# Seven half-size products for the second feed-forward matmul of a decoder layer, with sums formed by adding DMAs

## The chip, the core and the metric

The kernel runs on one core of one Trainium2 chip. TensorE (PE) multiplies, VectorE (DVE), ScalarE (ACT) and GpSimd (POOL) do the rest of the arithmetic, and DMAs are issued from the queues of SyncE (SP), POOL and, rarely, ACT. The metric is the device time of one execution in microseconds.

## The reference

One decoder layer on 1024 prompt tokens and 8 x 8 sampled tokens (1088 tokens in all), in float32, model width 1024, feed-forward width 2816:

```python
proj = rmsnorm(x, norm1_g) @ w_in            # q, k, v, glu_a, glu_b, gate_a, gate_b
branch_a = attend(q, k, v, mask, sinks) @ w_o_attn           # window 128, 16 heads
u = glu_a * jax.nn.sigmoid(glu_b)                            # conv module, 31 taps
branch_b = silu(layernorm(dwconv_valid(u_ext, conv_b_w, conv_b_bias))) @ w_pb
h = x + (sigmoid(gate_a) * branch_a + sigmoid(gate_b) * branch_b) @ w_out
up = rmsnorm(h, norm2_g) @ w_up                              # 1024 x 5632
gate, val = jnp.split(dwconv_valid(up_ext, ffn_conv_w, ffn_conv_b), 2, axis=-1)
y = h + (silu(gate) * val) @ w_down                          # 2816 x 1024, changed here
```

The outputs are the normed `y` and the new caches and conv states.

## The kernel before

Activations lie transposed: 128 channels on the partitions, tokens along the free axis. Every float32 operand is split into a rounded part and a rest (`h`, `l`; `split_ps` does it with one ACT copy and one DVE subtract), and a product is three matmuls (`mm3`): high by high, high by low, low by high. Weights come as units of 128 x 1024 from `wall` through two `wraw` buffers (`w_load`, on SP) and are split into `whi` and `wlo` (`w_split`).

The stages follow one another: norm and input projections (`phase_x`), 44 weight units in the order `SEQUENCE`, most of them a stream of 72 matmuls, with attention units woven in between by an agenda (`plan`, `tick`) and the 31-tap convolution as background work on DVE (`conv`); the projections of the two branches and their output (`phase_y`, `phase_z`); then the feed-forward. In its first product (`ffn_up`), channel groups 3 to 21 already use seven products of half size in place of eight: `plan_pair` forms the sums of weight blocks on DVE as it goes, and `pair` adds the results. Each group's gated result goes to DRAM (`d_g`, from POOL). The second product (`down`, `ffn_down`) takes the 22 groups in six lots (`GROUPS`), keeps the output `H` in SBUF and adds each lot to it; the last lot also does the final norm (`final`, `tail`).

The program's text gives a priority, not the order: the scheduler places each instruction on its engine's queue when it reckons that its inputs and its buffer are there, the text's order deciding among those that are ready, and `later` lowers the priority. An engine's queue then runs strictly in the order found. At most eight DMAs of SP and eight of POOL are under way, each queue by eight semaphores in turn. So a DMA without inputs, as one from an input tensor to DRAM, can be placed far ahead of its place in the text. Before the change one such pair of DMAs was tied down by hand:

```python
if f == 2:
    with tc.issue_after(z.ins):
        nc.gpsimd.dma_start(a["o_kwp"], a["kpT"][:, :, :, NT:])
        nc.gpsimd.dma_start(a["o_vwp"], a["vp"][:, NT:, :])
```

Names used below: `xl` the low half of the normed input, `u` the conv module's buffers (two), `gt` the gates' buffers (two) on their way to DRAM, `p` the softmax tiles (two), which a POOL copy of `nsink` opens.

Of the kernel before, what the change touches and what calls it, by code (L numbers as in the profile page):

```python
# [9 lines left out]
ALU = mybir.AluOpType  # L10
# [33 lines left out]
GROUPS = (2, 4, 4, 4, 4, 4)  # L44
# [29 lines left out]
def weight_order():  # L74
    order, count = [], {}
    gates = [(kind, i) for i in range(KT) for kind in ("ga", "gb")]
    for w in SEQUENCE:
        n = count[w] = count.get(w, -1) + 1
        if w == "g":
            order.append(gates.pop(0))  # L80
        elif w[0] == "q":
            order.append(("q", (int(w[1]), n)))
        elif w[0] == "k":
            order.append(("k", int(w[1])))
        else:
            order.append((w, n))
    assert not gates
    n_in = len(order)
    order += [("o", m) for m in range(KT)]
    order += [("pb", m) for m in range(KT)]  # L90
    order += [("out", m) for m in range(KT)]
    for f in range(NF):
        order += [("up", f), ("up", NF + f)]
    order += [("dn", f) for f in range(NF)]
    groups = [list(range(sum(GROUPS[:n]), sum(GROUPS[:n + 1]))) for n in range(len(GROUPS))]
    return order, groups, n_in
# [16 lines left out]
class Build:  # L113
    def __init__(self, tc, a):
        self.tc, self.nc, self.a = tc, tc.nc, a
        self.order, self.groups, self.n_in = weight_order()
# [18 lines left out]
    def w_load(self):  # L135
        i = len(self.w_raw)
        if i < len(self.order):
# [5 lines left out]
    def w_split(self):  # L143
        if len(self.w_hl) < len(self.order):
# [25 lines left out]
    def weight(self, what, ahead=1):  # L170
# [3 lines left out]
        while len(self.w_raw) < min(i + 3, len(self.order)):  # L174
# [358 lines left out]
    def run(self):  # L533
        nc, tc, a = self.nc, self.tc, self.a
        es = ExitStack()
        with es:
# [8 lines left out]
            self.d_g = self.t(dp, [NF, P, FW], "d_g")  # L545
# [22 lines left out]
    def derive(self):  # L568
# [7 lines left out]
        nc.vector.tensor_scalar(self.nsrow, self.c("srow", 0, 2), -1.0, None, ALU.mult)  # L576

# [3 lines left out]
    def phase_x(self):  # L581
# [222 lines left out]

        for n, (kind, i) in enumerate(self.order[:self.n_in]):
            if n < FIRST:
                continue
            if n == self.n_in - LAST_GATES:
# [66 lines left out]
    def phase_z(self, s_es, sh, sl):  # L875
# [102 lines left out]
        H, h_es = self.ffn_up(hh, hl, mp)  # L978
        m_es.close()
        self.ffn_down(H, h_es)  # L980


    def ffn_up(self, hh, hl, mp):
# [12 lines left out]
        first = n_up + 2 * PLAIN  # L996

# [3 lines left out]
        def raw_slot(i):  # L1001
            if first <= i < n_up + 2 * NF and (i - first) // 2 % 2:
                return ft, "wraw2"
            return self.wp, "wraw"

        def slot(i):
            if i < n_up:
                return old_slot(i)
            if i < first:
                return (ft, ("wraw2", "wraw2")) if i == first - 1 else (self.wp, (i - first) % 2)  # L1010
            return ((self.wp, ("wlo0", "whi1")), (ft, ("wraw2", "wraw2")))[i - n_dn]

        old_slot, self.slot = self.slot, slot
        self.raw_slot, self.w_stop = raw_slot, first
        gt = {}
# [23 lines left out]
        def up_conv(f, st, ss):  # L1039
            nc.gpsimd.tensor_copy(co[:, f, 0:2], st[:, SEQ:SEQ + 2])  # L1040
            nc.gpsimd.tensor_copy(co[:, f, 2:].rearrange("p (b t) -> p b t", b=NB), ss[:, :, NT:])
            acc = self.t(ft, [P, AW], "acc", bufs=3)
            nc.scalar.activation(acc, st[:, 0:AW], AF.Identity, bias=fb(f), scale=fw(f, 0))  # L1043
            for k in (1, 2):
                nc.vector.scalar_tensor_tensor(acc, st[:, k:k + AW], fw(f, k), acc, ALU.mult, ALU.add)  # L1045
            return acc

        def finish(f, both):
            with self.later(UP_LATER):
                ga = up_conv(f, *both[0][:2])  # L1050
                nc.scalar.activation(ga, ga, AF.Silu)
                va = up_conv(NF + f, *both[1][:2])
                nc.vector.tensor_tensor(va, va, ga, ALU.mult)
                nc.gpsimd.dma_start(self.d_g[f, :, 0:AW], va)
# [14 lines left out]
        def sums():  # L1069
            add = lambda o, x, y, op=ALU.add: nc.vector.tensor_tensor(o, x, y, op)  # L1070
            for j in range(2):
                for kk in range(0, KT // 2, 2):
                    ks = slice(kk, kk + 2)

                    def word(c, y):
                        r = self.t(ft, [P, 2, QW], "s", bufs=4)
# [4 lines left out]
                    add(r11, r12, r11, ALU.subtract)  # L1081
                    add(r12, r22, r12, ALU.subtract)
                    add(r22, r22, r11, ALU.subtract)
                    add(r21, r21, r22, ALU.subtract)
# [3 lines left out]

        ring = {"n": 0, "tiles": []}
# [5 lines left out]
        preps = []  # L1095

        def plan_pair(f):
            i = n_up + 2 * f
            hw = DM // 2
            live = {}  # L1100

            def raws():
                while len(self.w_raw) < min(i + 4, len(self.order)):
                    self.w_load()
                ra, rb = self.w_raw[i:i + 2]
                live.update(a11=ra[:, :hw], a12=ra[:, hw:], a21=rb[:, :hw], a22=rb[:, hw:])

            def make(name, x, y, op):
                def go():
                    s = live[name] = self.t(ft, [P, 2 * QW], "s", bufs=4)[:, :hw]  # L1110
                    nc.vector.tensor_tensor(s, live[x], live[y], op)
                return go

            def split(name, before=None):
                def go():
                    if name == "a11":
                        raws()
                    if before:
                        before()
                    w = self.t(self.wp, [P, DM], ("whi0", "wlo0", "whi1", "wlo1")[ring["n"] % 4], F32R, bufs=1)  # L1120
                    ring["n"] += 1
                    self.split_ps(w[:, :hw], w[:, hw:], live[name])
                    ring["tiles"].append((w[:, :hw], w[:, hw:]))
                return go

            preps.extend([
                split("a11"),
                split("s1", make("s1", "a21", "a22", ALU.add)),
                split("s2", make("s2", "s1", "a11", ALU.subtract)),
                split("s4", make("s4", "a12", "s2", ALU.subtract)),  # L1130
                split("s3", make("s3", "a11", "a21", ALU.subtract)),
                split("a12"), split("a22")])

        def prep(n):
            while ring["n"] < min(n, len(preps)):
                preps[ring["n"]]()

        def pair(f):
# [4 lines left out]
            plus = lambda d, s: nc.vector.tensor_tensor(d, d, s, ALU.add)  # L1143
            seq = [
                ("A", "11", True, pg, 0, copy), ("E", T1, True, pv, 2, copy), ("A", T2, False, pg, 2, copy),
                ("E", "22", False, pg, 2, plus), ("A", T3, False, pv, 2, plus), ("C", "21", True, pg, 0, plus),
                ("A", T4, False, pv, 0, copy)]
            for n, (bank, b, fresh, parts, c, op) in enumerate(seq):
                prep(base + n + 1 + AHEAD)
                if f == NF - 1 and n == 4:  # L1150
                    self.w_hl += [None] * (n_dn - len(self.w_hl))
                    self.w_stop = len(self.order)
                    for _ in self.groups[0]:
                        self.w_load()
                        self.w_split()
                wh, wl = ring["tiles"][base + n]
                for j in range(2):
# [8 lines left out]
                    for d, r in parts(c + j):  # L1166
                        op(d, r(ps))  # L1167
            finish(f, both)

        for f in range(PLAIN, NF):  # L1170
            plan_pair(f)
# [5 lines left out]
        self.w_used = self.order.index(("dn", 0))  # L1177
        for f in range(PLAIN, NF):
            pair(f)
            if f == NF - 4:  # L1180
                for x in self.groups[0]:
                    t = self.t(ft, [P, AW], "acc", bufs=3)[:, :T]
                    gt[x] = self.g_load(x, t, *(self.t(mp, [P, T], f"m{y}{2 + x}0", F32R) for y in "hl"))
        nc.gpsimd.dma_start(a["o_cf"], co)
        t_es.close()
        h_es = ExitStack()
        H = self.t(pool(h_es, "hd", "left"), [P, KT, T], "H")
        self.down(0, H, gt, None)
        f_es.close()
        return H, h_es  # L1190


    def g_load(self, f, va, h, l):
        self.nc.sync.dma_start(va[:, :SEQ], self.d_g[f, :, :SEQ])
        self.nc.sync.dma_start(va[:, SEQ:].rearrange("p (b t) -> p b t", b=NB),
                               self.d_g[f, :, SEQ + 2:].rearrange("p (b t) -> p b t", t=FROW)[:, :, :NT])
        self.split_ps(h, l, va)
        return h, l

    def down(self, n, H, gt, dt, ahead=None):  # L1200
        nc, g, last = self.nc, self.groups[n], n == len(self.groups) - 1
        ws = [self.weight(("dn", f), len(g) - 1 - x) for x, f in enumerate(g)]
        for c, (o, w) in enumerate(TAIL_CHUNKS if last else CHUNKS):
            if c == 1 and ahead:
                ahead()
            ssq = self.t(dt, [P, 384], "fssq", bufs=2) if last else None
            for m in range(KT):
                ms = slice(m * P, (m + 1) * P)
                ps = self.bank(("mm", "aux")[m % 2])
                for x, f in enumerate(g):  # L1210
                    h, l = gt[f]
                    self.mm3(ps[:, :w], ws[x][0][:, ms], ws[x][1][:, ms], h[:, o:o + w], l[:, o:o + w],
                             x == 0, x == len(g) - 1)
                hs = H[:, m, o:o + w]
                if n == 0:
                    nc.scalar.copy(hs, ps[:, :w])
                else:
                    nc.vector.tensor_tensor(hs, hs, ps[:, :w], ALU.add)
                if n == 1:
# [213 lines left out]
```

## Time and profile before

| what | value |
|---|---|
| time, median of 3 runs (lowest to highest) | 1707.12 us (1704.47 to 1707.89) |
| profiled execution: span from first to last instruction | 1704.2 us; its time outside the span is not given |
| PE busy | 1679.8 us, 11440 matmuls |
| DVE, ACT, POOL busy | 1281.4, 850.0, 246.4 us |
| moved by DMA | 172.18 MB, mean 101 GB/s |
| mean PE clock granted | 0.996 |

Busy time is the time in which an engine runs an instruction; matmuls overlap, so a busy PE says only that there are no gaps. DMA share is the part of the 16 DMA engines' time in which they move packets; in a short window it can read above 1. A copy from DRAM to DRAM counts its bytes once in GB/s. Line numbers are those of the kernel that the row belongs to.

### The profile page before, as it was taken

What the parts mean: (1) busy time and instruction counts of PE and PEld (TensorE: products, weight loads), DVE (VectorE), ACT (ScalarE), POOL (GpSimd) and SP (SyncE); (2) the same over time, 40 slices, a digit from 0 to 9 for tenths busy, and PEclk for the clock granted to TensorE, in tenths of its full rate; (3) what the DMA queues carried; (4) which work ended last, traced back from release to release, by engine and by line L of the source; (5) the groups of instructions that cost most, each with busy time, mean ns of one, the idle gap of its engine ahead of it and who ended that gap; (6) DMA issues with size and microseconds to landing.
All of it is one profiled execution on the core that took longest, in us unless ns stands there. A gap on an engine that the chain in (4) does not pass through costs nothing.

```text
span 1704.2 us, 29288 instructions
## 1 busy us (share of the span) xinstructions
PE 1679.8 (99%) x11440; PEld 1661.6 (98%) x11440; DVE 1281.4 (75%) x2253; ACT 850.0 (50%) x1729; POOL 246.4 (14%) x430
## 2 busy tenths in 40 slices
PE   9999999999999999999999999999999999999998
PEld 8999899999999999999999999999999999999998
DVE  8899999999579986755447977777777773754436
ACT  7534577733588736963233535444444455311112
POOL 1210112130011111100000441222222220000000
PEclk9999999999999999999999999999999999999999
DMA  6122213232211274553344132222222223853103
GB/s 208 42 51 79 65 46 113 80 123 63 75 44 56 76 255 144 172 172 125 122 131 135 53 123 77 77 77 77 77 77 77 90 66 125 271 140 103 52 1 106
DMA packets 104347, 172.18 MB, mean 101 GB/s; under 512 B 44512, under 2 KB 70512, under 8 KB 104192
## 3 DMA queue, kind: packets, MB, share of 16 engines
q1 hardware_dynamic: 90352, 124.88, 24.5%
q0 software_dynamic: 13424, 45.15, 7.4%
q8 instruction: 90, 1.47, 0.3%
q14 instruction: 49, 0.40, 0.1%
q10 hardware_dynamic: 432, 0.27, 0.1%
HBM read 124.74 MB, written 47.50 MB: 101 GB/s over the span
## 4 chain that ended last, share of the span: by engine, by line
PE 83%; DVE 10%; ACT 3%; issue 2%; DMA 1%; POOL 0%; SPq 0%; DVEq 0%; ACTq 0%; POOLq 0%
PE mm L182 20%; PE mm L184 20%; PE mm L183 20%; PE aux L184 6%; PE aux L183 6%; PE aux L182 6%; DVE c L456 2%; DVE bt L456 2%; PE aux L342 1%; PE aux L354 1%; PE aux L355 1%; PE aux L332 1%; PE aux L333 1%; DMA xr<-xT 1%; DVE wlo L164 1%
## 5 line engine op out<-in xcount | busy, mean ns | idle before, releaser
L182 PE MATMUL mm<-xh,whi 128*128 128x384 f32 (+1 forms) x920 | 306.3, 333 | 0.4 <-ACT whi L163 0.3
L183 PE MATMUL mm<-xl,whi 128*128 128x384 f32 (+1 forms) x920 | 300.7, 327 | 0.2 <-DVE xl L246 0.2
L184 PE MATMUL mm<-xh,wlo 128*128 128x384 f32 (+1 forms) x920 | 300.3, 327 | 0.0
L182 PEld LDWEIGHTS mm<-xh,whi 128*128 128x128 f32 x920 | 172.9, 188 | 2.0 <-ACT whi L163 0.9
L183 PEld LDWEIGHTS mm<-xl,whi 128*128 128x128 f32 x920 | 173.0, 188 | 1.6 <-DVE xl L246 0.7
L184 PEld LDWEIGHTS mm<-xh,wlo 128*128 128x128 f32 x920 | 172.7, 188 | 0.1
L163 ACT CAST whi<-wraw 128x1024 fp32r<-128x1024 f32 (+1 forms) x91 | 90.0, 993 | 161.6 <-PE aux L183 82.8
L164 DVE TENSOR_TENSOR wlo<-wraw,whi 128x1024 fp32r<-128x1024 f32 (+1 forms) x91 | 104.3, 1151 | 44.7 <-ACT whi L163 44.4
L1045 DVE SCALAR_TENSOR_TENSOR acc<-st,fc,acc 128x1104 f32<-128x1104 f32 x88 | 119.8, 1364 | 4.7 <-ACT acc L1043 3.9
L182 PE MATMUL mm<-mh,whi 128*128 128x272 f32 x368 | 106.6, 290 | 0.0
L183 PE MATMUL mm<-ml,whi 128*128 128x272 f32 x368 | 106.1, 288 | 0.0
L184 PE MATMUL mm<-mh,wlo 128*128 128x272 f32 x360 | 104.1, 289 | 0.0
L456 DVE SCALAR_TENSOR_TENSOR bt<-u,consts,bt 128x513 f32<-128x513 f32 x120 | 89.9, 750 | 0.6
L456 DVE SCALAR_TENSOR_TENSOR c<-sm,hsum,c 128x512 f32<-128x512 f32 x120 | 89.6, 747 | 0.6
L456 DVE SCALAR_TENSOR_TENSOR c<-u,consts,c 128x512 f32<-128x512 f32 x112 | 83.6, 747 | 0.2
L182 PE MATMUL mm<-gh,whi 128*128 128x384 f32 (+3 forms) x240 | 78.1, 326 | 3.4 <-ACT gh L211 3.4
L183 PE MATMUL mm<-gll,whi 128*128 128x384 f32 (+3 forms) x240 | 78.5, 327 | 0.7 <-DVE gll L212 0.7
L184 PE MATMUL mm<-gh,wlo 128*128 128x384 f32 (+3 forms) x240 | 78.5, 327 | 0.0
L184 PE MATMUL aux<-gh,wlo 128*128 128x384 f32 (+3 forms) x240 | 78.2, 326 | 0.0
L183 PE MATMUL aux<-gll,whi 128*128 128x384 f32 (+3 forms) x240 | 78.2, 326 | 0.0
L182 PE MATMUL aux<-gh,whi 128*128 128x384 f32 (+3 forms) x240 | 78.0, 325 | 0.0
L182 PE MATMUL mm<-th,whi 128*128 128x272 f32 x240 | 70.1, 292 | 2.4 <-ACT st L1167 2.2
(382 smaller groups left out, 5292.0 us busy)
## 6 DMA issues: line engine op xcount, KB each, us to landing
wraw<-wall SPq DMA_DIRECT2D x131, 512.0 KB, 4.0
d_g<-acc POOLq DMA_DIRECT2D x22, 552.0 KB, 5.1
gr<-d_g SPq DMA_DIRECT2D x20, 512.0 KB, 5.2
ga<-d_ga SPq DMA_DIRECT2D x8, 544.0 KB, 4.5
gb<-d_gb SPq DMA_DIRECT2D x8, 544.0 KB, 3.7
mar<-d_ma SPq DMA_DIRECT2D x8, 544.0 KB, 5.6
xr<-xT SPq DMA_DIRECT2D x32, 136.0 KB, 2.4
d_h<-H POOLq DMA_DIRECT2D x4, 1088.0 KB, 5.9
```

What stands on the lines that cost most here:

```text
L163: self.nc.scalar.copy(h[:, z], r[:, z])
L164: self.nc.vector.tensor_tensor(l[:, z], r[:, z], h[:, z].bitcast(F32), ALU.subtract)
L182: mm(ps, wh, xh, start=first, stop=False, skip_group_check=more)
L183: mm(ps, wh, xl, start=False, stop=False, skip_group_check=more)
L184: mm(ps, wl, xh, start=False, stop=last, skip_group_check=more)
L332: nc.tensor.matmul(ps[:, j, :], q[g][:, h, qs], kd[g][:, keys], start=True, stop=False)
L333: nc.tensor.matmul(ps[:, j, :], q[g][:, h, qs], kl[g][:, keys], start=False, stop=True)
L342: nc.tensor.transpose(ps[:, h * P:(h + 1) * P], pt[:, h, kb * P:(kb + 1) * P], self.ident)
L354: nc.tensor.matmul(av, v, ph, start=kb == kbs[0], stop=False)
L355: nc.tensor.matmul(av, v, pl, start=False, stop=kb == kbs[-1])
L456: mac = lambda o, x, w: nc.vector.scalar_tensor_tensor(o, x, w, o, ALU.mult, ALU.add)
L1045: nc.vector.scalar_tensor_tensor(acc, st[:, k:k + AW], fw(f, k), acc, ALU.mult, ALU.add)
```

## The change

Of the 22 groups of the second product, 20 are taken as 10 pairs. A pair's 256 x 1024 weights are cut in 2 x 2 blocks (group by half of the columns), the 256 x 1088 operand in 2 x 2 blocks (group by half of the tokens), and seven products of sums of blocks replace the eight of blocks. The ten pairs run in four rounds (`ROUNDS`) of 2, 3, 3 and 2 pairs; in each round, four blocks of 128 output columns (and the same in the other half) take seven products of 272 columns twice. The last two groups go as before.

The weight sums are no longer formed on DVE but by DMA, for both products: `folds` copies blocks of `wall` to the seven slots of a pair in DRAM (SP) and then adds blocks in three steps (POOL, `accum_op`). The text steps it once per stream of the input projections for the first product (`d_wu`, 19 pairs) and once per group of the feed-forward for the second (`d_wd`, 10 pairs). The operand's sums are formed in `finish` by one DVE sum and adding DMAs into `d_x`. The results of the rounds are added by DMA to `h` in DRAM (`d_h`), from where `H` is loaded for the last two groups and the final norm.

```diff
-GROUPS = (2, 4, 4, 4, 4, 4)
+ROUNDS = ((0, 1), (2, 3, 4), (5, 6, 7), (8, 9))
+NP = 10
+LAST = (20, 21)
+HT = T // 2
+FOLD_FROM = 8
...
+    def folds(self, out, units):
...
+        def put(eng, n, x, slots, **kw):
+            d = out[7 * n + slots.start:7 * n + slots.stop:slots.step or 1].rearrange("x p c -> p x c")
+            eng.dma_start(d, x[:, None, :].to_broadcast([P, d.shape[1], hw]), **kw)
...
+        def plain(n):
+            a, b, c, d = of(n)
+            put(sync, n, a, slice(0, 1))
+            put(sync, n, a, slice(2, 5))
+            put(sync, n, d, slice(1, 7, 5))
+            put(sync, n, b, slice(5, 6))
+
+        def add(n, which, slots):
+            put(gpsimd, n, of(n)[which], slots, accum_op=ALU.add)
+
+        steps = (plain, lambda n: add(n, 2, slice(1, 5)), lambda n: add(n, 3, slice(2, 4)), lambda n: add(n, 1, slice(3, 4)))
+        count = out.shape[0] // 7
+        for at in range(count + len(steps) - 1):
+            for k, step in enumerate(steps):
+                if 0 <= at - k < count:
+                    step(at - k)
+            yield
...
+        folds = self.folds(self.d_wu, lambda n: (n_up + 2 * (n + PLAIN), n_up + 2 * (n + PLAIN) + 1, False))
         for n, (kind, i) in enumerate(self.order[:self.n_in]):
...
+            if n >= FOLD_FROM:
+                next(folds, None)
...
         def finish(f, both):
...
-                nc.gpsimd.dma_start(self.d_g[f, :, 0:AW], va)
...
+                nc.vector.tensor_tensor(s, o[:, :HT], o[:, HT:], ALU.add)
+                x = self.d_x[f // 2].rearrange("x p t -> p x t")
+                halves = o.rearrange("p (x t) -> p x t", x=2)
+                if f % 2:
+                    nc.gpsimd.dma_start(x[:, 5:7], halves)
+                    nc.gpsimd.dma_start(x[:, 2:5:2], o[:, None, HT:].to_broadcast([P, 2, HT]), accum_op=ALU.add)
+                    nc.gpsimd.dma_start(x[:, 3], s, accum_op=ALU.add)
+                else:
+                    nc.gpsimd.dma_start(x[:, 0:5:4], halves)
+                    nc.gpsimd.dma_start(x[:, 1:4], s[:, None, :].to_broadcast([P, 3, HT]))
...
+        def load_two():
...
+                nc.sync.dma_start(r.rearrange("p (x c) -> p x c", x=n), self.d_wu[2 * d:2 * d + n].rearrange("x p c -> p x c"))
...
+                nc.sync.dma_start(l.bitcast(F32).rearrange("p (x c) -> p x c", x=7),
+                                  self.d_wd[f:f + 7, :, m * P:(m + 1) * P].rearrange("x p c -> p x c"))
...
+        folds = self.folds(self.d_wd, lambda n: (n_dn + 2 * n, n_dn + 2 * n + 1, True))
         for f in range(PLAIN, NF):
-            pair(f)
+            next(folds, None)
+            pair(f, hook)
...
+            for n, (bank, fresh) in enumerate((("A", 1), ("E", 1), ("A", 0), ("E", 0), ("A", 0), ("C", 1), ("A", 0))):
...
+                        self.mm3(ps, wh[:, ws], wl[:, ws], x[:, :HT][:, js], x[:, HT:][:, js],
+                                 bool(fresh) and i == 0, i == len(blk[r, m]) - 1, not fresh)
...
+                    nc.gpsimd.dma_start(self.d_h[row, :, half * HT:(half + 1) * HT], ev[d], accum_op=ALU.add)
```

The order on SP right after the load of u for the second conv group. Before (`wraw_948` is the weight unit of the eighth stream):

```order
L603 DMA u_944<-cbT 128x8x30
L140 DMA wraw_948<-wall 128x1024
L140 DMA wraw_1039<-wall 128x1024
L803 DMA masks_942<-masks 128x640
L140 DMA wraw_1187<-wall 128x1024
```

After (`wraw_952` is the same unit; the first row here is the last of 23 copies that stand between it and u_948):

```order
L593 DMA d_wu_64<-wall 128x2x512
L145 DMA wraw_952<-wall 128x1024
L593 DMA d_wu_64<-wall 128x512 x2
L593 DMA d_wu_64<-wall 128x3x512
L145 DMA wraw_1043<-wall 128x1024
```

Plain copies of `d_wu` stand between the weight loads from here on, up to eight ahead of each; all 76 are placed before wraw_2038, the load that was wraw_1991.

The order on POOL where the first softmax tiles are opened (the two copies from `nsink`). Before:

```order
L630 DMA o_cbp<-u_1492 128x30
L631 DMA o_cbs<-u_1492 1024x1x30
L480 DMA d_c_59<-u_944 128x64
L479 DMA d_c_59<-u_944 128x1024
L722 DMA o_vp<-gt_1959 128x256
L601 MEMSET u_2381 128x30
L602 MEMSET u_2381 128x2
L298 COPY p_1998<-nsink_81 128x4
```

After, in a row from the same output DMA of the third u buffer to the same copy:

```order
L671 DMA o_cbp<-u_1511 128x30
L672 DMA o_cbs<-u_1511 1024x1x30
L593 DMA d_wu_64<-wall 128x512
L593 DMA d_wu_64<-wall 128x2x512
L593 DMA d_wu_64<-wall 128x512 x2
L485 DMA d_c_59<-u_948 128x64
L484 DMA d_c_59<-u_948 128x1024
L763 DMA o_vp<-gt_1992 128x256
L642 MEMSET u_2442 128x30
L643 MEMSET u_2442 128x2
L303 COPY p_2045<-nsink_85 128x4
```

All 57 adds into `d_wu` stand ahead of that copy, the first of them right after the first gate write at the kernel's start.

The order on PE where the stream of the next weight unit begins (`mm_2391` before, `mm_2452` after, writing its first PSUM bank). `kd`, `kl`, `q` are the keys and queries of attention scores, `pth` and `ptl` the turned softmax tile, `sp` the softmax tile of the sampled tokens being turned, `av` the result. Before:

```order
L405 MATMUL aux_2413<-consts_74,sp_2345 128x128
L406 MATMUL aux_2413<-consts_74,sp_2345 128x128
L182 MATMUL mm_2391<-xh_17_101,whi_216_2188 128x384
L183 MATMUL mm_2391<-xl_18_102,whi_216_2188 128x384
L184 MATMUL mm_2391<-xh_17_101,wlo_217_2189 128x384
L332 MATMUL aux_2424<-kd_139_1378,q_23_119 128x256
L333 MATMUL aux_2424<-kl_141_1380,q_23_119 128x256
```

After:

```order
L359 MATMUL aux_3983<-pth_3929,v_945 128x512
L360 MATMUL aux_3983<-ptl_3930,v_945 128x512
L410 MATMUL aux_4031<-consts_78,sp_3948 128x128
L411 MATMUL aux_4031<-consts_78,sp_3948 128x128
L418 MATMUL aux_4058<-av_4034,vs_2020 128x128
L421 MATMUL aux_4058<-av_4034,vp_3940 128x64 x2
L187 MATMUL mm_2452<-xh_21_105,whi_220_2242 128x384
```

The stream now begins behind the last attention matmul of the first half of the heads; 272 attention matmuls stand ahead of it in one block, where before they were spread over eight streams.

392 lines of the change are left out of this document (243 added, 149 removed).

## The prediction

> **What bounds the kernel now.** I read the page first (busy times, slices, chain), then the stages by windows, then the DMA answers and the queues' timelines.
>
> ```profile
> span 1704.2 us, 29288 instructions
> PE 1679.8 (99%) x11440; PEld 1661.6 (98%) x11440; DVE 1281.4 (75%) x2253; ACT 850.0 (50%) x1729; POOL 246.4 (14%) x430
> ...
> PE 83%; DVE 10%; ACT 3%; issue 2%; DMA 1%; POOL 0%; SPq 0%; DVEq 0%; ACTq 0%; POOLq 0%
> ```
>
> PE is busy 99% of the span and 83% of the chain that ended last; DVE has 10% of that chain, DMA 1%. So matmuls taken away come off the time, and any wait put in front of PE goes on top of it. Now the stages. The columns are window, length, then each engine's busy time with its instructions, PE clock, DMA share, GB/s.
>
> ```profile
> 28.00:189.00 161.00, 159.37 (x1048) 158.94 (x1047) 152.33 (x242) 68.76 (x140) 27.35 (x37) 1.00 0.21 55
> ...
> 1200.00:1402.00 202.00, 202.00 (x1607) 202.00 (x1606) 154.61 (x231) 99.44 (x190) 44.53 (x85) 1.00 0.24 79
> 1447.00:1470.00 23.00, 20.60 (x101) 20.27 (x102) 17.49 (x23) 9.34 (x10) 0.00 (x0) 0.85 0.82 254
> 1470.00:1670.00 200.00, 199.98 (x1226) 199.69 (x1225) 103.73 (x167) 38.47 (x44) 0.00 (x0) 1.00 0.34 97
> ```
>
> The input projections (28 to 189), the first feed-forward product (1200 to 1402, 272 columns a matmul) and the second (1470 to 1670, up to 384 columns) all run PE without gaps. DMA looks idle: a share of 0.21 to 0.34. The change spends exactly that idle share, so what matters is when.
>
> **The change, part by part.**
>
> *Matmuls.* In the second product 1452 matmuls go (864 of 384 columns, 432 of 320, 96 of 352, 48 of 256, 12 of 512), and 1680 of 272 come (10 pairs x 4 column blocks x 7 products x 2 halves x 3). By the rows above a matmul of this stage takes 200/1226 = 0.163 us and one of 272 columns 202/1607 = 0.1257 us: 1452 x 0.163 = 237, 1680 x 0.1257 = 211, so 26 us less. The stage's start also goes: in 1447 to 1470 only 101 matmuls ran, 16.5 us of work in 23, at a clock of 0.85; the new code prepares round 0 earlier. That is up to 6.5 us more. I take -32 (from -26 to -33).
>
> *The folds before attention.* `folds` writes the seven weight sums of 19 + 10 pairs to DRAM. One pair takes 4 plain copies on SP (7 x 256 KB) and 3 adding DMAs on POOL (another 7 x 256 KB). The code spreads the first 19 pairs over the input projections and puts the other 10 into the feed-forward, but the order shows them elsewhere: all 76 plain copies of `d_wu` stand on SP between u_948 and wraw_2038, 23 of them ahead of wraw_952, and all 57 adds stand on POOL ahead of the first L303 copy that opens the softmax. Those places have times in the trace of before:
>
> ```profile
> 27.24 0.55 SPq L603 DMA_DIRECT2D u<-cbT  x1
> 68.05 4.44 SPq L140 DMA_DIRECT2D wraw<-wall  x2
> ...
> 149.01 18.04 SPq L140 DMA_DIRECT2D wraw<-wall  x3
> ```
>
> ```profile
> 188.96 1.74 POOL L298 COPY p<-nsink 128x4 f32<-128x4 f32 x2
> ```
>
> So 19 x 7 x 262144 bytes = 34.9 MB are copied and 34.9 MB added between about 28 and 189 us: 161 us. Behind the queued folds wait, on SP, the weight loads of the projections (23 copies, 10 MB, are ahead of the one issued at 68 us), and on POOL the `xl` halves of the norm, the spills of `u`, the gate writes and the softmax copies; PE waits for all of these. What the DMA engines can carry:
>
> ```profile
> 10.00:20.00 10.00, 9.56 (x51) 8.43 (x50) 7.91 (x20) 8.33 (x19) 0.16 (x2) 1.00 1.00 351
> ...
> 988.00:990.00 2.00, 2.00 (x18) 2.00 (x17) 2.00 (x3) 0.80 (x3) 1.81 (x2) 1.00 1.37 436
> ```
>
> 351 GB/s with all engines busy, 436 in the best 2 us. And a copy on one queue slows a load on the other; the first fence is 984 to 996 us, where two DRAM-to-DRAM copies of POOL run beside two weight loads, the second the median over the program:
>
> ```profile
> wraw<-wall SPq DMA_DIRECT2D x2, 512.0 KB, 10.4
> o_kwp<-kpT POOLq DMA_DIRECT2D x1, 960.0 KB, 7.2
> o_vwp<-vp POOLq DMA_DIRECT2D x1, 960.0 KB, 10.8
> ```
>
> ```profile
> wraw<-wall SPq DMA_DIRECT2D x131, 512.0 KB, 4.0
> ```
>
> A load took 10.4 us instead of 4.0, so the queues share. Demand in those 161 us, in us of all 16 engines: the old traffic 0.21 x 161 = 34, the copies 34.9 MB / 0.351 = 99, the adds 99 times a factor. No adding DMA is in the trace. At the least an add costs what a copy costs (factor 1): 34 + 99 + 99 - 161 = 71 us late. [...] With factor 1 at the best 2 us' rate: 34 + 80 + 80 - 161 = 33. [...]
>
> [...] No run here shows an add yet.
>
> *Attention without filler.* In before, 272 attention matmuls of the first half of the heads are woven into eight streams of 72 matmuls. In after the order puts these 272 in one block ahead of mm_2452, because that stream's weights stand far back on SP. The stretch, and the ACT work in it:
>
> ```profile
> 226.00:355.00 129.00, 128.96 (x836) 125.05 (x834) 124.28 (x277) 98.47 (x246) 30.46 (x61) 1.00 0.30 96
> ```
>
> ```profile
> L309 ACT ACTIVATE p<-p,nm 128x257 f32<-128x257 f32 x48 | 24.0, 502 | 4.7 <-DVE nm L304 4.6
> L313 ACT ACTIVATE p<-p,den 128x256 f32<-128x256 f32 x48 | 20.5, 499 | 0.5 <-DVE den L311 0.4
> L211 ACT CAST pth<-aux 128x512 fp32r<-128x512 f32 x24 | 13.5, 579 | 6.1 <-PE aux L354 4.8 <-DVE ptl L212 1.1
> L309 ACT ACTIVATION_READ_ACCUMULATOR p<-p,nm 128x1 f32 x48 | 9.0, 187 | 0.0
> ...
> L360 ACT COPY av<-aux 64x512 f32<-64x512 f32 x12 | 7.0, 581 | 6.1 <-PE aux L355 5.7
> ```
>
> Alone, attention takes at least ACT's 24.0 + 20.5 + 13.5 + 9.0 + 7.0 = 74 us, at most the 129 it has now. The streams then take 564 x 0.163 = 92 us by themselves. 74 + 92 - 129 = +37, 129 + 92 - 129 = +92; I take +55, nearer to ACT's sum, since softmax has two `p` buffers.
>
> *The folds of the second product.* 40 copies (18.4 MB, 52 us) and 30 adds (52 to 105 us) stand between the weight loads and gate writes of those eight streams. With old traffic of 0.30 x 92 = 27 and about 10 us of copies already done beside attention: 52 + 27 + 52 - 10 - 92 = 29 late at factor 1, 82 at 2. Nothing needs these sums until the feed-forward, so only the gate writes queued among the adds (two `gt` buffers) hold PE: 0 to +82, I take +25.
>
> *The feed-forward.* First product: 133 half-size sums are loaded ready-made, which takes 76 DVE sums away; finish adds three products and one sum on DVE and ten `d_x` transfers per pair on POOL. DVE is at 155 of 202 us there, and PE never waits: nothing, as long as `st` (4 buffers, now held until its DMA has read it) comes back within a pair's 21 us. Second product: 70 loads of x (19.5 MB), 40 of weights in 512-byte rows (18.3 MB), 64 adds into `d_h` (17.8 MB) in some 225 us. At 351 GB/s, with the o_kwp row's 0.98 MB in 7.2 us for such short rows and factor 1.5: 56 + 134 + 76 = 266 us of engine time at the worst, 56 + 52 + 51 = 159 at the best. So 0 to +40; I take +10. The splits (about 1 us each on ACT and DVE) hide behind blocks of 84 or 126 matmuls (10.6 and 15.9 us). The end of the kernel keeps its form: nothing.
>
> *Sum.* -32 + 121 + 55 + 25 + 10 = +179 on the span of 1704.2. The page gives no time outside the span; the three times are 1704.5 to 1707.9, so at most 4 us lie around it. On the median, 1707.1: **1886 us**. Low ends: -33 + 33 + 37 = +37, 1744. High ends: -26 + 170 + 92 + 82 + 40 = +358, 2065.
>
> **The rivals.**
>
> *The DMA engines keep up, and it is faster.* The place is the first copy into `p`. It decides at the rate where 69.8 MB fit beside the old traffic, 69.8 / (161 - 34) = 550 GB/s. Then only the attention block stays, and if ACT's rows get shorter once PE and DVE stop interfering (60 us instead of 74), it costs 23: -32 + 23 = -9, **1698 us**. For it: a DMA share of 0.21. Against: no window over 436 GB/s. 10%.
>
> *Adds at the price of copies, at burst rate.* Everything else as forecast, at its low ends: 1744 to 1785. For it: 436 GB/s was in a DRAM-to-DRAM stretch. 17%.
>
> *Adds three times as dear,* each waiting for the one before it in its pair: 34 + 99 + 297 - 161 = 269 us late, and 82 in the second batch: -32 + 269 + 55 + 82 + 10 = +384, 2091. POOL's queue would then be the bound until attention ends. 14%.
>
> *That the change doesn't do what it says* shows no sign: the order has the 1680 matmuls. 1%.
>
> **How the numbers follow.** Forecast 58%, the rivals 10, 17, 14 and 1%. The range, 1735 to 2060, holds the forecast with its unknown costs, the second rival, and the cheaper part of the third; what is left out is the faster case and most of the dear adds. About 0.2% is what a measurement of this kernel can tell: faster 10%, within it 2%, slower 88%.
>
> **What would show it.** Right: in the slices PE below 9 in the first quarter of the span and DMA at 9 there; the first copy into `p` at 260 to 360 us instead of 189; POOL waiting for its own DMAs on the fold line; a stretch of some 80 to 110 us with attention alone on PE; the second product at 0.126 us a matmul and some 25 us shorter. Wrong: PE at 9 through the first 400 us, or an add that lands like a copy. If the first quarter holds and the end is late, the sizes for the second product were wrong.

## The result, and the profile after

The changed kernel takes 2097.09 us (median of 4 runs, 2084.22 to 2107.66) against 1706.61 before: 1.2289 times as long, 95% interval 1.2237 to 1.2342. The forecast was slower, 1886 us, but the range ended at 2060.

First the page of the changed kernel: span, engines, slices (each 53 us here), queues and the chain by line.

```profile
span 2105.9 us, 30429 instructions
PE 1723.6 (82%) x11668; PEld 1688.9 (80%) x11668; DVE 1266.5 (60%) x2221; ACT 906.8 (43%) x1833; POOL 393.1 (19%) x609
PE   8655235666733799999999999999999999888986
PEclk9877668767967899999999999999999999999998
DMA  9999999222999721126444334365555558979784
q1 hardware_dynamic: 149888, 211.44, 32.6%
q0 software_dynamic: 55968, 131.62, 30.7%
PE 56%; DMA 28%; issue 6%; ACT 5%; DVE 4%; POOL 1%; SPq 1%; DVEq 0%; POOLq 0%; ACTq 0%
```

PE fell from 99% to 82% of the span and DMA rose from 1% to 28% of the chain. The slices show where: PE is below 9 in the first 14 slices, and DMA stands at 9 in slices 1 to 7 and 11 to 13; then PE runs full until the last six slices, which are the second product. The queue q0 is POOL's, q1 that of SP; a row of a queue gives packets, MB, and the share of the 16 engines' time.

Next the stretches of the changed kernel by window (columns as before): up to the first softmax copy, attention, the streams behind it, the first product, the second.

```profile
28.00:383.00 355.00, 175.12 (x1074) 172.51 (x1072) 158.08 (x257) 70.43 (x143) 88.61 (x94) 0.75 1.02 227
383.00:513.00 130.00, 92.40 (x450) 78.46 (x450) 95.50 (x257) 95.84 (x273) 19.98 (x48) 0.75 0.15 47
520.00:748.00 228.00, 134.97 (x766) 133.75 (x766) 95.92 (x137) 30.45 (x51) 50.81 (x64) 0.78 0.95 206
1310.00:1760.00 450.00, 447.37 (x3542) 447.13 (x3541) 317.07 (x431) 219.42 (x366) 120.59 (x216) 1.00 0.51 151
1780.00:2060.00 280.00, 239.85 (x1713) 232.92 (x1713) 128.23 (x208) 117.97 (x233) 54.53 (x64) 0.93 0.85 196
```

The work that took 161 us now takes 355, with the DMA engines full (1.02). Attention stands nearly alone in the second row: from 413.9 to 515.9 us PE runs attention matmuls and nothing else. The streams behind it take 228 us with PE busy for 135 of them, beside nearly full DMA engines again (0.95). The first product is as it was; the second runs PE at 86%.

The first softmax copy, and who waited where, from POOL's timeline and the waits of the changed kernel (columns of a wait: total us, times, longest):

```profile
376.85 0.81 POOL L593 DMA_DIRECT2D d_wu<-wall  x1 [5.17 <-DMA d_wu<-wall]
...
382.91 0.32 POOL L303 COPY p<-nsink 128x4 f32<-128x4 f32 x2
```

```profile
POOL d_wu L593 <- DMA d_wu<-wall: 229.6, 37, 15.6
...
POOL d_wd L593 <- DMA d_wd<-wall: 124.1, 17, 16.6
```

The copy comes at 382.9 us instead of 188.96, 6 us behind the last add into `d_wu`. Four places on the time axis split the loss and serve for all experiments below: the first copy into `p`, the first gated result `ma` of phase y, the last copy of a conv state into `co` (end of the first product), and the end of the span. The last column is the time from that conv state to the end, the second product with the final norm. The time is the median of a kernel's runs, the places are those of its one profiled execution. With untied folds the runs of one kernel spread (changed 2084 to 2108, e2 2068 to 2081, e7 2041 to 2067), so differences of places between such kernels hold to some 20 us only.

| kernel | time us | first p | phase y | first product's end | second product |
|---|---|---|---|---|---|
| before | 1706.6 | 189.0 | 651.3 | 1418.7 | 285.5 |
| changed | 2097.1 | 382.9 | 1008.8 | 1773.8 | 332.1 |
| e1: folds add nothing | 2009.0 | 321.3 | 911.7 | 1675.0 | 331.0 |
| e2: second folds tied | 2074.8 | 372.6 | 897.1 | 1754.1 | 325.4 |
| e3: no folds | 1826.1 | 249.7 | 711.7 | 1488.9 | 332.1 |
| e4: e3 with long rows | 1808.5 | 250.2 | 712.3 | 1489.8 | 317.5 |
| e6: e3 with d_wl tied | 1762.7 | 189.8 | 652.0 | 1430.6 | 330.4 |
| e11: e6 with copies into d_h | 1719.4 | 188.1 | 651.7 | 1430.9 | 285.2 |
| e5: e11 with long rows | 1710.9 | 189.9 | 652.0 | 1430.0 | 277.3 |
| e7: changed, d_wl tied | 2054.1 | 410.3 | 945.6 | 1712.0 | 327.4 |
| e8: folds paced on SP | 1956.6 | 220.2 | 778.2 | 1627.7 | 327.4 |
| e9: paced on SP and POOL | 1885.3 | 210.3 | 703.9 | 1550.3 | 333.0 |
| e10: before, plus d_wl | 1765.1 | 248.1 | 710.1 | 1476.2 | 284.7 |

Of the 401.7 us between the two spans, 193.9 are lost by the first `p`, 163.6 from there to phase y, 46.6 in the second product, and 2.4 are gained between.

### The profile page after: what moved, and what is told of

Read it like the earlier page. It is cut to its first block, busy times and chain, and to the rows that moved or that the text cites. A ratio compares the mean times of both kernels' runs of the same rounds, so it can differ in the third digit from the quotient of the medians.

```text
span 2105.9 us, 30429 instructions
## 1 busy us (share of the span) xinstructions
PE 1723.6 (82%) x11668; PEld 1688.9 (80%) x11668; DVE 1266.5 (60%) x2221; ACT 906.8 (43%) x1833; POOL 393.1 (19%) x609
## 3 DMA queue, kind: packets, MB, share of 16 engines
HBM read 263.38 MB, written 189.34 MB: 215 GB/s over the span
## 4 chain that ended last, share of the span: by engine, by line
PE 56%; DMA 28%; issue 6%; ACT 5%; DVE 4%; POOL 1%; SPq 1%; DVEq 0%; POOLq 0%; ACTq 0%
PE mm L187 14%; PE mm L188 13%; PE mm L189 13%; DMA d_wu<-wall 12%; DMA d_wd<-wall 6%; PE aux L187 4%; PE aux L189 3%; PE aux L188 3%; DMA wl<-d_wd 3%; ACT p L314 1%; DMA d_c<-u 1%; DMA wlo<-d_wd 1%; PE aux L347 1%; DMA wraw<-d_wd 1%; ACT p L318 1%
## 5 line engine op out<-in xcount | busy, mean ns | idle before, releaser
L169 DVE TENSOR_TENSOR wlo<-wraw,whi 128x1024 fp32r<-128x1024 f32 (+1 forms) x71 | 80.0, 1131 | 150.3 <-ACT whi L168 149.9
L168 ACT CAST whi<-wraw 128x1024 fp32r<-128x1024 f32 (+1 forms) x71 | 69.0, 977 | 203.4 <-PE mm L188 117.4
L189 PE MATMUL mm<-th,wlo 128*128 128x272 f32 x486 | 141.3, 291 | 0.0
L187 PE MATMUL mm<-th,whi 128*128 128x272 f32 x486 | 140.9, 290 | 0.0
L187 PE MATMUL mm<-mh,whi 128*128 128x272 f32 x462 | 135.4, 293 | 6.2 <-ACT ev L1361 3.5
L188 PE MATMUL mm<-tl,whi 128*128 128x272 f32 x474 | 137.8, 291 | 0.0
L189 PE MATMUL mm<-mh,wlo 128*128 128x272 f32 x462 | 134.7, 291 | 0.0
L216 ACT CAST whi<-wraw 128x1024 fp32r<-128x1024 f32 (+1 forms) x67 | 69.8, 1042 | 132.6 <-PE aux L188 72.8
L593 POOL DMA_DIRECT2D d_wu<-wall x57 | 64.5, 1225 | 245.4 <-DMA d_wu<-wall 229.6
L347 PE MATMUL aux<-consts,p 128*128 128x128 f32 x240 | 46.8, 322 | 64.2 <-ACT p L318 64.2
L217 DVE TENSOR_TENSOR wlo<-wraw,whi 128x1024 fp32r<-128x1024 f32 (+1 forms) x67 | 81.4, 1215 | 29.7 <-ACT whi L216 29.7
L347 PEld LDWEIGHTS aux<-consts,p 128*128 128x128 f32 x240 | 34.1, 161 | 74.5 <-ACT p L318 70.0
```

What stands on the lines that cost most here:

```text
L168: self.nc.scalar.copy(h[:, z], r[:, z])
L169: self.nc.vector.tensor_tensor(l[:, z], r[:, z], h[:, z].bitcast(F32), ALU.subtract)
L187: mm(ps, wh, xh, start=first, stop=False, skip_group_check=more)
L188: mm(ps, wh, xl, start=False, stop=False, skip_group_check=more)
L189: mm(ps, wl, xh, start=False, stop=last, skip_group_check=more)
L216: self.nc.scalar.copy(h, src)
```

## The experiments

**What an add costs (e1).** The steps of `folds` that add become copies:

```diff
-            put(gpsimd, n, of(n)[which], slots, accum_op=ALU.add)
+            put(gpsimd, n, of(n)[which], slots)
```

> The adding DMAs of the folds are plain copies of the same blocks on the same queue (the weight sums are not formed). Theory A, the add is dear because it also reads its target: in the changed kernel's first 400 us POOL's queue took 54.9% of the engines' time for 38.07 MB (5.8 us per MB), SP's 42.3% for 50.59 MB (3.3 us per MB). With 3.3 for all 69.8 MB the demand before attention is 34 + 233 us in 161: +106 in place of +194, first copy into p at about 295 us, and the second batch shorter by about 45: about 1965 us. Rival Q, POOL's queue itself is slow, whatever it moves: first copy into p at 375 to 390 us, total 2080 to 2105.

Measured: first copy at 321.3 us, total 2009.03 (ratio to the kernel before 1.1779, 95% interval 1.1756 to 1.1803; so below). Between the two theories, nearer to A. The DMA queues from 40 to 320 us (packets, MB, share of 16 engines), the changed kernel first, then e1:

```profile
q0 software_dynamic: 15270, 30.11, 62.4%
q1 hardware_dynamic: 18176, 34.95, 42.5%
```

```profile
q1 hardware_dynamic: 19693, 39.55, 47.9%
q0 software_dynamic: 10231, 36.95, 45.2%
```

In 280 us, POOL's adds take 0.624 x 280 / 30.11 = 5.8 us of all engines per MB, its copies 0.452 x 280 / 36.95 = 3.4, and SP's transfers 3.4 in both. So the queue is not slow; the add is, by 1.7 times. Why it is dearer is not shown: the page counts the same bytes read in both kernels (263.38 MB), so it does not tell whether an add reads its target. What it does show is that an add moves in more packets, 507 per MB against 277. The copy at 321 us instead of the expected 295 stays open too: the engines were busy for 0.93 of this window in e1, against 1.05 in the changed kernel, so part of the time is not theirs; the order is that of the changed kernel still, and POOL still waits for its own transfers.

**Where the second folds stand (e2).** The 10 pairs of `d_wd` are tied behind the weight loads of the feed-forward:

```diff
-            next(folds, None)
+            with tc.issue_after(self.tie.ins):
+                next(folds, None)
             pair(f, hook)
```

> The folds of the second product's weights are tied behind the weight loads of the feed-forward, where the text has them; the first 19 pairs stay as they are. First copy into p at about 383 us either way. Theory A, the eight streams after attention were late through these folds alone (520 to 748 us for some 94 us of work, 134 late), and the feed-forward has DMA time for them (share 0.5 of 475 us, and 167 more): phase y's first result at about 875 us in place of 1008.8, total about 1963. Rival S, the folds cost as much wherever they are, since gate writes or operand writes queue behind them: phase y as early, but the feed-forward longer by 100 to 160 us, total 2070 to 2100. What is left at phase y over before, less the 194 ahead of attention, is the price of attention without filler; predicted +55.

Measured: phase y at 897.1, 112 us earlier than in the changed kernel, 10 of them already there at the first `p`: so these folds cost about 101 us in their old place. But the total fell by only 22, to 2074.84: the stretch from phase y to the first product's end got 92 us longer. Rival S holds, with a loss a little under its 100 to 160. The waits of e2 from 1200 to 1600 us show how:

```profile
POOL d_wd L593 <- DMA d_wd<-wall: 188.8, 21, 13.4
ACT st L1041 <- DMA d_x<-st: 92.4, 9, 13.5
...
PE aux L187 <- ACT st L1041: 60.1, 8, 9.7
```

POOL waits for its own folds with the operand's transfers into `d_x` queued behind; these hold the `st` buffers, ACT cannot empty a bank, PE waits. What remains at phase y, 897.1 - 651.3 less the 183.6 us of delay at the first `p`, is 62 us: the price of attention without filler.

**No folds at all (e3, e4).** Blocks of the weights stand in for the sums; for the second product 20 units are first copied to DRAM (10.5 MB, two per pair of the first product). In e4 each weight load of the second product is one row of 3584 bytes per partition:

```diff
-                nc.sync.dma_start(l.bitcast(F32).rearrange("p (x c) -> p x c", x=7),
-                                  self.d_w2[f:f + 7, :, m * P:(m + 1) * P].rearrange("x p c -> p x c"))
+                nc.sync.dma_start(l.bitcast(F32), self.d_w2[2 * ROUNDS[r][i] + m % 2, :, :7 * P])
```

> No folds at all: blocks of the weights themselves are loaded in place of the sums, in transfers of the same shapes (2 KB rows in the first product, 512-byte rows in the second). Theory A: first copy into p at 189 us as before, phase y at 651, the first product unchanged, the second product as slow as in the changed kernel (from the last conv state of the first product to the end 331 us against 286): about 1752 us. Rival P, the second product was slow only through what the folds left behind (clock, late sums): 1675 to 1690.

> As the kernel without folds, and the weights of the second product come in rows of 3584 bytes in place of seven of 512 (which blocks they are is not the reference's choice). Theory R, the short rows make each block's load 7 to 10 us long and PE waits for them: the loads land in 2 to 4 us and the second product is at 0.126 us a matmul: 1680 to 1695 us. Rival H, the adding DMAs into d_h or the loads of x hold it: within 15 us of the kernel without folds, about 1740 to 1755.

Measured: 1826.14 (1.0703, 1.0687 to 1.0719) and 1808.48 (1.0592, 1.057 to 1.0614). The second product is as slow without folds as with them (332.1), as theory A of e3 had it, so it has a cost of its own. Long rows give back only 15 us there: theory R is wrong, since the loads hardly land faster (median 6.9 us against 7.4). But e3's total is 74 us above theory A's 1752, and 61 us of that are lost, in both kernels, where nothing had been expected: the first `p` came at 249.7. The timelines of SP and of ACT in e3:

```profile
26.58 0.57 SPq L643 DMA_DIRECT2D u<-cbT  x1
27.20 0.66 SPq L1286 DMA_DIRECT2D d_wl<-wall  x1
72.31 0.33 SPq L843 DMA_DIRECT2D masks<-masks  x1
72.83 0.81 SPq L145 DMA_DIRECT2D wraw<-wall  x2
129.14 0.56 SPq L643 DMA_DIRECT2D u<-cbT  x1
```

```profile
125.19 0.76 ACT L471 ACTIVATE bt<-u,consts 128x513 f32<-128x513 f32 x1 [28.38 <-DVE u L483]
...
134.20 1.97 ACT L168 CAST whi<-wraw 128x1024 fp32r<-128x1024 f32 x2
```

The same stretch of SP in the kernel before:

```profile
92.53 50.58 SPq L140 DMA_DIRECT2D wraw<-wall  x5
143.29 0.55 SPq L603 DMA_DIRECT2D u<-cbT  x1
```

The text's copy of the last two weight units, `d_wl`, stands at 27 us in e3. Behind it the order has changed: the load of a conv buffer (129 us) now stands ahead of the five weight loads that it followed before, and on ACT the conv's `bt` stands ahead of the weight split and waits 28 us for DVE (before, its `bt` at 139.5 us followed the splits at 99, 112 and 125). PE, with no split weights, stands still until then: it is busy for 0.5 us of the 30 from 100 to 130 us.

**That one copy (e6, e7, e10).** It is tied to its place, in e6 without folds and in e7 in the changed kernel; e10 is the kernel before with the copy added and nothing else.

```diff
-        nc.sync.dma_start(self.d_wl, a["wall"][n_dn + LAST[0]:n_dn + NF])
+        with tc.issue_after(self.tie.ins):
+            nc.sync.dma_start(self.d_wl, a["wall"][n_dn + LAST[0]:n_dn + NF])
```

> As the kernel without folds (512-byte rows), and the one copy into d_wl is tied to its place in the feed-forward. Theory L: that copy alone, placed on SP at 27 us, moved two loads of conv buffers ahead of the weight loads and the conv's ACT work ahead of the weight splits, so that PE stood still from 100 to 150 us; the order is now that of before up to the feed-forward, so the first copy into p comes at 189 us, phase y at 651, total 1826 - 61 = about 1765. Rival: the 61 us come from the transfer itself or from the changed timing of something else, and most of them stay: 1810 to 1826.

> The changed kernel with only the copy into d_wl tied to the feed-forward. Theory A, the folds' traffic sets the start whatever the order is: first copy into p still at 370 to 385 us, total 2070 to 2100. Rival L, the 61 us that this copy costs without folds are part of the 194: first copy at about 322 us, total about 2036.

> The kernel before, and nothing else changed but one more copy of the last two weight units (1 MB, DRAM to DRAM) at the text's place in the feed-forward, not tied; nothing reads it. The order puts it on SP right after the second conv buffer's load, at about 27 us, with the same shifts as in the kernel without folds. Theory L: it costs what tying it gave there, about +61 us: 1765 us. Rival: that was an effect of both together, and the copy alone costs its transfer at most: 1705 to 1712 us.

Measured: e6 1762.65 (1.0337, 1.0318 to 1.0355), first `p` at 189.8, phase y at 652.0; e10 1765.06 (1.0345, 1.033 to 1.0361), first `p` at 248.1. Theory L holds in both directions: a 1 MB copy that nobody reads costs 59 us by where the scheduler puts it. e10's waits from 70 to 160 us name the same place, and its window shows PE busy for 10 of 60 us:

```profile
PE mm L182 <- ACT whi L163: 34.8, 1, 34.8
ACT bt L466 <- DVE u L478: 28.4, 1, 28.4
```

```profile
90.00:150.00 60.00, 10.20 (x58) 9.43 (x57) 59.97 (x90) 5.81 (x7) 2.73 (x6) 0.59 0.08 16
```

In e7 neither expectation was right. The total fell by 43 to 2054.05, but the first `p` came later, at 410.3, and phase y 63 us earlier. With the copy gone from its place behind the folds (it was issued at 320.9 us in the changed kernel), PE's order has the attention matmuls woven into the streams again. So the block of 272 attention matmuls hung on this copy too. Its price is 62 us by e2. The 63 of e7 are not a second measurement of it: there the adds of the second folds begin at 362 us, before the first `p`, instead of at 529, so the 63 are what weaving and this shift come to together.

**The adds into d_h (e11, e5).** Base is e6; e11 copies instead of adding, e5 has the long rows of e4 as well.

```diff
-                    nc.gpsimd.dma_start(self.d_h[row, :, half * HT:(half + 1) * HT], ev[d], accum_op=ALU.add)
+                    nc.gpsimd.dma_start(self.d_h[row, :, half * HT:(half + 1) * HT], ev[d])
```

> As the kernel without folds and with the copy into d_wl tied (512-byte rows, 1762.65 us), with only the adding DMAs into d_h made plain copies of the same size (the rounds are not summed). With long rows as well it took 1710.93. Theory H, the adds alone are the loss and the short rows cost nothing once the engines are free: 1711 to 1720 us. Rival R, the short rows (14 us with the adds in place) stay a cost of their own: 1722 to 1735.

> As the kernel without folds and with long rows, with two edits in different stages: the 1 MB copy of the last two weight units into d_wl is tied to its place in the feed-forward, and the adding DMAs into d_h are plain copies of the same size (the rounds are not summed). The second product is counted from the last conv state of the first product to the end: 286 us before, 331 in the changed kernel, 317 with long rows. Theory H, the adds into d_h fill the DMA engines (39.9% of 310 us for 18.24 MB, 6.8 us per MB, and a block's load lands in 6.9 us however long its rows are): as copies they take half, loads land sooner, PE does not wait: 255 to 270 us. Rival V, ACT's queue is the limit: it waits for a weight load with the bank copies behind it, and that stays: over 300 us. In all, about 1690 by H, 1730 by V, if the early stage is as before.

Measured: e11 1719.38 (1.0077, 1.0061 to 1.0094), e5 1710.93 (1.003, 1.0019 to 1.0042); the second product 285.2 and 277.3 us. Of the 52 us between e6 and e5, 43 are the adds and 8.5 the rows; e11 lies within theory H's 1711 to 1720, and the rows are still worth something, as R had it. For e5 neither forecast was met: 277.3 us lies between theory H's 255 to 270 and rival V's over 300, and the total of 1710.93 between their 1690 and 1730. The queues in the second product of e6 (330 us) and of e11 (285 us):

```profile
q0 software_dynamic: 9296, 18.24, 36.9%
...
d_h<-ev POOLq DMA_DIRECT2D x60, 272.0 KB, 6.5
wl<-d_w SPq DMA_DIRECT2D x23, 448.0 KB, 7.8
```

```profile
q0 software_dynamic: 5200, 18.24, 16.9%
...
d_h<-ev POOLq DMA_DIRECT2D x60, 272.0 KB, 4.2
wl<-d_w SPq DMA_DIRECT2D x23, 448.0 KB, 5.7
```

The same 18.24 MB take 122 us of all engines as adds (6.7 per MB) and 48 as copies (2.6): 2.5 times. An add again moves in more packets than a copy, 9296 for the queue against 5200. A weight load lands in 7.8 and 5.7 us. How this reaches PE is seen in the waits of the second product, of e6 and then of e11:

```profile
ACT wh L216 <- DMA wl<-d_w: 43.5, 19, 7.6
PE aux L187 <- ACT ev L1037: 28.3, 16, 6.4
```

```profile
ACT wh L216 <- DMA wl<-d_w: 21.4, 23, 2.7
PE aux L187 <- ACT ev L1037: 1.7, 2, 1.2
```

ACT waits for a weight block with the copies out of PSUM (`ev`) behind it on its queue, and PE waits for the bank. With copies in place of adds ACT's wait halves and PE's goes from 28.3 to 1.7 us. In the changed kernel the same two waits are 38.8 and 21.8 us.

Even e5's second product is only 8 us shorter than before, not 32. PE is busy for 252 us of it against 275 before, so the matmuls give 22; but it stands still for 25 us against 11. The end shows most of that, before (first row) and in e5:

```profile
1670.00:1704.20 34.20, 27.48 (x197) 25.71 (x195) 19.87 (x47) 8.61 (x23) 0.00 (x0) 0.97 0.29 100
1660.00:1707.30 47.30, 30.51 (x194) 28.48 (x192) 31.79 (x74) 14.36 (x35) 0.00 (x0) 0.84 0.41 140
```

About as many matmuls take 13 us longer there. PE waits 7.1 us of that for the final norm's sums on DVE, for which it did not wait before; what holds the rest is not shown.

**Pacing the folds (e8, e9).** Both leave nothing out: all 29 pairs are stepped behind every second weight load from the eighth on, `d_wl` is tied, and PE's order up to phase y is that of before (behind it some 70 matmuls stand otherwise). e9 ties the adds on POOL as well:

```diff
+            if i >= FOLD_FROM and i % 2 == 0 and self.folding:
+                y = self.nc.gpsimd.tensor_copy(self.t(self.wp, [P, 1], "tie", bufs=2), r[:, 0:1])
+                with self.tc.issue_after(z.ins), self.tc.issue_after(y.ins):
+                    next(self.folding, None)
```

> The changed kernel whole, with all 29 pairs of folds tied behind every second weight load from the eighth on, and the copy into d_wl tied. PE's order is that of before up to the feed-forward. Theory A: a pair takes 7 x 0.262 MB x (3.3 + 5.8) = 16.7 us of the engines every 24 to 26 us, beside a share of 0.21 to 0.30: they fit (0.9), nothing is late by more than 20 us up to the feed-forward, and what is left is the first product's +10 and the second's +46: 1755 to 1790 us. Rival C, at 0.9 the loads and the gate writes queue behind the folds, as POOL waits for its own adds: 50 to 150 us more, 1820 to 1900.

> As the paced kernel, and the adding DMAs are tied as well: on POOL they follow a one-column copy of the weight unit just loaded, so that a step of adds stands on the queue some 25 us behind the transfers that it builds on. Nothing is left out. Theory W, the paced kernel lost its 190 us to POOL, which waited 598 us in all for transfers of its own folds with gate writes, spills and softmax copies queued behind: these waits fall below 150 us, phase y comes at 660 to 690 us in place of 778, the feed-forward at about 960, total 1765 to 1800. Rival D, the DMA engines' load (mean share 0.74 up to the feed-forward, loads in 5.8 us) is what delays, however the queue stands: phase y at 760 or later, total 1900 to 1960.

Measured: e8 1956.63 (1.1485, 1.142 to 1.1551), e9 1885.28 (1.106, 1.1042 to 1.1079). Waits of e8 up to the feed-forward, then the windows of e9 in phases y and z:

```profile
POOL d_wu L598 <- DMA d_wu<-wall: 368.3, 46, 16.9
POOL d_wd L598 <- DMA d_wd<-wall: 229.5, 24, 15.0
ACT gt L698 <- DMA d_gb<-gt: 71.9, 9, 26.1
```

```profile
800.00:900.00 100.00, 86.11 (x471) 83.98 (x470) 41.51 (x72) 44.73 (x72) 17.35 (x21) 0.90 0.82 213
900.00:1000.00 100.00, 84.53 (x537) 83.55 (x536) 36.77 (x77) 24.07 (x49) 14.50 (x16) 0.93 1.00 253
```

In e8 POOL waits 598 us for its own transfers and the gate writes stand behind them, as rival C had it, but the total is 57 us above C's range. In e9 these waits are gone from the list, and phase y comes at 703.9 instead of 778.2 us, near theory W's 660 to 690 and far from rival D's 760. POOL has other waits in their place, at the ties, up to 1100 us:

```profile
POOL tie L148 <- DMA wraw<-wall: 254.8, 27, 29.5
```

From phase y to the first product's end e9 takes 846 us against 767 before, and the loss lies in phases y and z. The DMA share there is 1.00 in one window and 0.81 from 700 to 1100 us, and POOL waits at its ties (the row above); which of the two holds PE is not shown. The total lies between the forecasts of W and D. No run takes the second folds into the first product, where the changed kernel's DMA share is 0.51, with their adds tied. No repair that keeps the folds came near the kernel before, and e5, with the sums for nothing and the adds at a copy's price, is still 0.3% above it. Its stand-in copies beside the first product cost some 11 us: from phase y to the first product's end e5 takes 778.0 us, before 767.4, and e7, which has no such copies, 766.4. Without them, by this estimate, e5 would lie about 0.3% below the kernel before. So the runs point to no version that is clearly faster than both, and none was made.

## Why the prediction was wrong

The direction was right, and so was the mechanism up to attention: folds placed ahead of attention, the DMA engines full there, the first `p` late, attention alone on PE, a second loss beside the gate streams. What failed are three terms of the sum: the DMA rates behind the *folds before attention* (+121, measured +193.9), the choice of +25 for the *folds of the second product* (measured about 101), and -32 + 10 for the second product (measured +46.6). Together they were 218 us too small; the whole sum, +179 on the span, was 223 us below the measured 401.7.

- *Folds before attention*, +121, measured +193.9. The form of the sum holds; two rates in it were wrong. The copies were put at 351 GB/s, from a window of loads into SBUF; between two places in DRAM and under load they ran at 3.4 us per MB, 294 GB/s. An add was put at 1.5 times the copy, 4.3 us per MB (34 + 99 + 149 - 161 = 121); it took 5.8. With the measured rates the same sum gives 34 + 34.9 x (3.4 + 5.8) - 161 = 194. That it meets the measured delay to within 1 us is luck in part: the same sum with 3.4 for both, which is e1, puts the first `p` at 299 us (measured 321.3), and in e7 the same folds in another order brought it at 410.3. The end of the range, 170, used a factor of two on the too fast copy. The factors 1.5 and 2, here and in the two terms of the second product, were the author's assumptions, and no run shows them; the runs showed 1.7 for the folds (e1) and 2.5 for `d_h` (e6 against e11).
- *Attention without filler*, +55, measured 62 by e2: right. PE had attention alone for 102 us, within the 74 to 129 of the working, and 102 + 92 - 129 = 65. Its cause was only half named; without the copy into `d_wl` the order weaves attention in again even with all folds in place (e7).
- *Folds of the second product*, +25 of 0 to 82, measured about 101 (e2). The working had it at 82 with a factor of two, and with the measured rates it gives 27 + 18.4 x (3.4 + 5.8) - 10 - 92 = 94; taking 25, on the ground that only the gate writes hold PE, was the error. Those held PE 93 us, as the changed kernel's waits from 520 to 748 us show:

```profile
PE mm L187 <- ACT gt L692: 93.0, 4, 44.2
ACT gt L692 <- DMA d_gb<-gt: 65.9, 4, 53.9
```

- *The second product*, -32 + 10 = -22, measured +46.6. Of the -32, 26 were matmul time, and e5 shows 22 of them. The 6.5 us of the stage's start did not come (PE idle for 5 of e5's first 50 us, for 4 of 51 before), and "the end of the kernel keeps its form: nothing" was wrong: it takes 13 us longer in e5. The DMA part was mis-sized: its worst case put the adds at 1.5 x 2.85 us per MB, and they took 6.7. "The splits hide" failed in the same place: a split waits for its load (38.8 us in the changed kernel), and the copies out of PSUM stand behind it. Adds and short rows together cost 52 us (e6 against e5).
- *The first product*, nothing, measured -2.4: right.
- *The rivals.* "Adds three times as dear" gave 2091 and the measured time is 2097; that it came so near is luck. Its adds before attention are 297 us of engine time, and 34.9 MB at the measured 5.8 are 202. It put the first delay at 269 us, measured 193.9, and had the second product 22 us shorter, measured 46.6 longer; the errors cancel. Its reason, adds that wait for one another, no run shows by itself: POOL does wait 229.6 us for its own folds, but the engines were full meanwhile. In "the DMA engines keep up", ACT's rows were to get shorter without filler; the rows L309 of 502 ns before (L314 after) take 500 in the block.

## What to carry to other kernels

Price a DMA in engine time per MB from a row with the same two memories and the same load, not from the best window: here 351 GB/s in a window of loads into SBUF stood against 294 between two places in DRAM under load. An adding DMA took 1.7 and 2.5 times a copy in the two places measured here. An idle DMA share is no room by itself: a transfer that waits in order on a queue makes everything behind it wait, as POOL's 598 us in e8 show. After adding any DMA without inputs, compare the whole order on each engine: a 1 MB copy that nothing read cost 59 us, and one line tied it down.

## What the hardware showed unexpected

PE's granted clock was low where PE waited. In a stretch of the changed kernel where PE stood almost still, it is 0.50; from 1310 to 1760 us, with PE busy for 447 of 450, it is 1.00; the mean of the profiled execution is 0.903:

```profile
250.00:300.00 50.00, 1.17 (x4) 1.17 (x5) 0.00 (x0) 1.64 (x5) 9.98 (x12) 0.50 0.98 225
```

The changed kernel and e5 run the same number of matmuls, in 1723.6 and 1660.6 us of busy time, at mean clocks of 0.903 and 0.992. How much of the 63 us is clock is not shown: e7 at 0.918 has 1699.9 us, and e9 at 0.956 has 1711.3. No run here shows what sets the clock.
